# Ragged layer norm: per-batch tiles replaced by fixed tiles, gathered row pairs and scattered zeros

## Chip, cores, metric

One core of one Trainium2 chip. The metric is device time in microseconds (us), median over executions.

## The reference

```python
batch, max_seq, dim = (32, 512, 1024)
lengths = np.random.randint(64, max_seq, size=batch)
...
output = np.zeros_like(x)
for b in range(batch):
    seq_len = lengths[b]
    x_b = x[b, :seq_len].copy()
    mean = np.mean(x_b, axis=-1, keepdims=True)
    var = np.var(x_b, axis=-1, keepdims=True)
    output[b, :seq_len] = (x_b - mean) / np.sqrt(var + eps) * gamma + beta
```

Inputs and output are 32-bit floats; a row of 1024 is 4 KB. The draw is fixed: the lengths sum to 9,274 of 16,384 rows. The rest of the output must be zero.

## The kernel before

It works batch by batch: 512 rows as four groups of 128 partitions. Two groups are always loaded, the third and fourth only where the length asks for them. All four are computed; rows past the length get a scale of zero, and all 512 rows are stored.

```python
def st_load(b):
    ...
    nc.sync.dma_start(out=xs[:, 0 : G - 2, :], in_=xr[:, 0 : G - 2])
    nc.sync.dma_start(out=xs[:, G - 2, :], in_=xr[:, G - 2], cond=rv > (G - 2) * P)
    nc.sync.dma_start(out=xs[:, G - 1, :], in_=xr[:, G - 1], cond=rv > (G - 1) * P)
# per batch: bn_stats/bn_aggr on VectorE, sqrt on ScalarE, 1/std * mask and -mean/std on VectorE,
# h = x*rstd + nmr on ScalarE (16 bit), h *= gamma on VectorE,
# identity matmul of h plus (mask x beta) matmul into PSUM, one 128x2048 copy out on ScalarE
def st_store(b):
    ...
    for hf in range(NH):
        pool.dma_start(
            out=out[b].rearrange("(g p) d -> p g d", p=P)[:, hf * H : hf * H + H],
            in_=osb_q[b][hf][:, :, :],
        )
# the last three batches take a path without TensorE (NTAIL = 3)
```

## Time and profile before

| | before |
|---|---|
| median of the first 5 runs | 314.99 us (314.52 to 316.15) |
| span of the profiled run | 313.4 us |
| moved by DMA | 117.14 MB in 30,703 packets |
| ScalarE / VectorE busy | 86% / 83% |
| GB/s, 80 to 150 us | 420 |

The span runs from the first to the last instruction of the profiled execution; "DMA share" is the mean busy share of the core's 16 DMA engines and can exceed 1 where packets overlap. The lines of the page are in the prediction below, with how to read them.

### The profile page before, as it was taken

How to read it: one execution, taken by the hardware profiler on the slowest of the kernel's cores; microseconds unless marked ns; L12 is line 12 of the kernel's file. 1: busy time of each engine (PE TensorE's matmuls, PEld its weight loads, DVE VectorE, ACT ScalarE, POOL GpSimd, SP SyncE). 2: the span in 40 equal slices, each digit the busy share in tenths (PEclk: the TensorE clock that was granted, in tenths of full speed). 3: DMA queues.
4: the chain of work that ended last, by engine and by line, in shares of the span. 5: the costliest groups of instructions: out<-in, count | busy, mean ns of one | idle time of the engine just before them, and what ended most of it. 6: DMA issues, size and time to landing. Idle time of an engine off the chain costs nothing.

```text
span 313.4 us, 2482 instructions
## 1 busy us (share of the span) xinstructions
PE 212.5 (68%) x465; PEld 51.7 (16%) x465; DVE 260.1 (83%) x630; ACT 268.6 (86%) x231; POOL 52.6 (17%) x74
## 2 busy tenths in 40 slices
PE   0001433888888899888867888898688769845800
PEld 0000100222222222222211222122122212111200
DVE  4399999999999999999889987989797699716410
ACT  1007669999999999999889999998999899999990
POOL 8000001111111111111111111011111011131230
DMA  6999955999999999999999999999999997678987
GB/s 209 418 362 331 357 208 197 356 367 367 419 419 421 419 422 419 418 423 419 418 422 421 420 419 421 420 420 421 419 419 421 420 385 279 268 280 321 387 319 298
DMA packets 30703, 117.14 MB, mean 374 GB/s; under 512 B 2128, under 2 KB 2128, under 8 KB 30688
## 3 DMA queue, kind: packets, MB, share of 16 engines
q0 software_dynamic: 17440, 67.15, 53.3%
q1 hardware_dynamic: 13248, 49.84, 40.6%
q14 instruction: 12, 0.10, 0.1%
q8 instruction: 3, 0.05, 0.1%
HBM read 68.19 MB, written 67.11 MB: 432 GB/s over the span
## 4 chain that ended last, share of the span: by engine, by line
issue 56%; DVE 18%; POOL 12%; DMA 9%; ACT 2%; PE 1%; POOLq 1%; SPq 0%; ACTq 0%
POOL out_dram L275 12%; DVE stats L147 6%; DVE stats L148 6%; DMA out_dram<-o_sb 5%; DVE h_sb L203 4%; DMA x_all<-in_x_dram 3%; ACT h_sb L190 1%; DVE mv L149 1%; PE ps L219 1%; ACT o_sb L263 1%; POOLq L275 0%; POOLq L344 0%; DVE rstd L170 0%; DVE nmr L174 0%; SPq L59 0%
## 5 line engine op out<-in xcount | busy, mean ns | idle before, releaser
L219 PE MATMUL ps<-h_sb,idn_h 128*128 128x512 f16 x232 | 108.8, 624 | 70.5 <-ACT o_sb L263 46.9
L190 ACT ACTIVATE h_sb<-x_all,nmr,rstd 128x1024 f16<-128x1024 f32 x128 | 148.5, 1244 | 6.1 <-DVE nmr L174 6.1
L263 ACT ACTIVATE o_sb<-ps 128x2048 f32<-128x2048 f32 x58 | 106.5, 1878 | 6.8 <-DMA out_dram<-o_sb 6.7
L229 PE MATMUL ps<-beta_h,maskr 1*128 1x512 f16 x232 | 109.0, 622 | 0.0
L147 DVE BATCH_NORM_STATS2 stats<-x_all 128x6 f32<-128x512 f32 x128 | 86.3, 674 | 16.4 <-DMA x_all<-in_x_dram 16.4
L203 DVE TENSOR_TENSOR h_sb<-h_sb,gamma_h 128x1024 f16<-128x1024 f16 x128 | 82.5, 675 | 14.4 <-ACT h_sb L190 14.4
L275 POOL DMA_DIRECT2D out_dram<-o_sb x64 | 45.3, 708 | 243.0 <-ACT o_sb L263 185.1
L148 DVE BATCH_NORM_STATS2 stats<-x_all 128x6 f32<-128x512 f32 x128 | 84.0, 656 | 0.0
L219 PEld LDWEIGHTS <-idn_h 128*128 128x128 f16 x232 | 27.1, 128 | 149.6 <-issue 91.9
L229 PEld LDWEIGHTS <-maskr 1*128 1x128 f16 x232 | 24.4, 125 | 80.8 <-issue 80.8
L156 ACT ACTIVATE sq<-mv,eps_sb 128x4 f32<-128x4 f32 x32 | 9.5, 303 | 22.6 <-DVE mv L149 17.2
L149 DVE BATCH_NORM_AGGREGATE mv<-stats 128x2 f32<-128x12 f32 x128 | 25.3, 197 | 0.2
L251 ACT ACTIVATE o_sb<-h_sb,maskt 128x1024 f32<-128x1024 f16 x12 | 12.8, 1143 | 0.0
L109 PE MATMUL mtp<-idn_f,maskt 128*128 128x128 f32 x1 | 0.4, 444 | 15.3 <-DVE maskt L98 15.3
L207 DVE TENSOR_TENSOR h_sb<-h_sb,beta_h 128x1024 f16<-128x1024 f16 x12 | 8.3, 692 | 0.4
L170 DVE RECIPROCAL rstd<-sq 128x4 f32<-128x4 f32 x32 | 5.4, 168 | 3.5 <-ACT sq L156 3.5
L61 POOL MEMSET x_all<- 128x6144 f32 x1 | 5.2, 5218 | 0.3 <-POOLq L330 0.3
L174 DVE SCALAR_TENSOR_TENSOR nmr<-mv,rstd 128x4 f32<-128x4 f32 x32 | 4.7, 148 | 0.0
L79 DVE CAST lenf<-len 128x32 f32<-128x32 int32 x1 | 2.3, 2298 | 2.8 <-DMA len<-in_lengths_dram 2.8
L171 DVE TENSOR_TENSOR rstd<-rstd,maskt 128x4 f32<-128x4 f32 x32 | 4.6, 144 | 0.0
L109 PEld LDWEIGHTS mtp<-idn_f,maskt 128*128 128x128 f32 x1 | 0.2, 183 | 15.3 <-issue 15.3
L117 POOL DMA_DIRECT2D maskr<-masktr x1 | 0.7, 692 | 9.7 <-DVE masktr L113 9.7
(18 smaller groups left out, 6.3 us busy)
## 6 DMA issues: line engine op xcount, KB each, us to landing
out_dram<-o_sb POOLq DMA_DIRECT2D x64, 1024.0 KB, 12.4
x_all<-in_x_dram SPq DMA_DIRECT2D x30, 1024.0 KB
x_all<-in_x_dram SPq DMA_DIRECT2D x60, 512.0 KB
x_all<-in_x_dram SPq DMA_DIRECT2D x2, 2048.0 KB
gamma_f<-in_gamma_dram SPq DMA_DIRECT2D x1, 512.0 KB
beta_f<-in_beta_dram SPq DMA_DIRECT2D x1, 512.0 KB
len<-in_lengths_dram SPq DMA_DIRECT2D x1, 32.0 KB
maskr<-masktr POOLq DMA_DIRECT2D x1, 32.0 KB, 6.2
```

Of the source, the lines that this page charges most:

```text
L147: dve.bn_stats(out=stats[:, g, 0, :], in_=xg[:, 0 : D // 2])
L148: dve.bn_stats(out=stats[:, g, 1, :], in_=xg[:, D // 2 : D])
L149: dve.bn_aggr(out=mv[:, g, :], in_=stats[:, g].rearrange("p a b -> p (a b)"))
L156: act.activation(out=sq[:, :], in_=mv[:, :, 1], func=AF.Sqrt, bias=eps_sb[:, 0:1], scale=1.0,)
L190: act.activation(out=h_sb[b][:, g, :], in_=x_all[:, b % NBX, g, :], func=AF.Identity, bias=nmr[:, g : g + 1], scale=rstd[:, g : g + 1],)
L203: dve.tensor_tensor(out=hg, in0=hg, in1=gamma_h[:, :], op=OP.mult)
L207: dve.tensor_tensor(out=hg, in0=hg, in1=beta_h[:, :], op=OP.add)
L219: pe.matmul(ps[:, i, c * CH : (c + 1) * CH], idn_h[:, :], h_sb[b][:, g, c * CH : (c + 1) * CH], start=True, stop=False,)
L229: pe.matmul(ps[:, i, c * CH : (c + 1) * CH], maskr[0:1, b * G + g, :], beta_h[0:1, c * CH : (c + 1) * CH], start=False, stop=True,)
L251: act.activation(out=o_sb[:, i, :], in_=h_sb[b][:, g, :], func=AF.Copy, bias=0.0, scale=maskt[:, b, g : g + 1],)
L263: act.activation(out=o_sb[:, :, :].rearrange("p a b -> p (a b)"), in_=pst[hf][:, :, :].rearrange("p a b -> p (a b)"), func=AF.Copy, bias=0 ...
L275: pool.dma_start(out=out[b].rearrange("(g p) d -> p g d", p=P)[:, hf * H : hf * H + H], in_=osb_q[b][hf][:, :, :],)
```

## The change

The intent: touch only rows that count. The first 64 rows of every batch exist whatever the lengths, so they are loaded as eight fixed tiles of 256 rows (two adjacent rows per partition). All further valid rows are numbered as row pairs over all batches; VectorE computes from the running sum of the lengths which pair lies in which partition, and GpSimd gathers and scatters 128 pairs (1 MB) at a time. Padding is written by scattering one tile of zeros. Engines branch on the number of tiles. Instead of a tile framework's dependencies the kernel keeps its own semaphores. The diff replaces nearly the whole file; this is its core, with cuts marked by dots and remarks after # added here:

```diff
-        nc.sync.dma_start(out=xs[:, 0 : G - 2, :], in_=xr[:, 0 : G - 2])
-        nc.sync.dma_start(out=xs[:, G - 2, :], in_=xr[:, G - 2], cond=rv > (G - 2) * P)
-        nc.sync.dma_start(out=xs[:, G - 1, :], in_=xr[:, G - 1], cond=rv > (G - 1) * P)
...
+                    for t in range(NST):                      # 8 fixed tiles, SyncE
+                        e.dma_start(out=xt[t][:, :], in_=st_view(x, t)).then_inc(s_xs[t], 16)
...
+                    def load(t):                              # GpSimd
+                        d = t - NST
+                        e.indirect_dma_start(
+                            out=xt[t % RX][:, :], out_offset=None, in_=xu,
+                            in_offset=bass.IndirectOffsetOnAxis(ap=idx_i[:, d : d + 1], axis=0), ...
+                    def store(t):
+                        wait(tok["evac", t])
...
+                    KJ = [2, 3, 4, 5, 6, 10, 14, 18, 22]      # zero scatter j goes out in step KJ[j]
+                    while len(KJ) < NZ:
+                        KJ.append(27 + (len(KJ) - 9) // 2)
...
+        for k in range(NSTEP):
+            if k >= 2:
+                dve_mul(k - 2)
+            if k >= 1:
+                dve_smalls(k - 1)
+            dve_stats(k)
...                                                            # index, mask and zero arithmetic
+            if k >= 1:
+                act_xn(k - 1)
+            if k >= 2:
+                pe_mm(k - 2)
+                act_evac(k - 2)                                # two 128x1024 copies, scale = mask
+            act_sqrt(k)
...
+                    e.reg_mul(rz, rz, 16)
+                    e.wait_ge(s_zero, rz)                      # all zero scatters landed
+                    e.drain()
```

In step k VectorE takes the statistics of tile k, ScalarE normalises tile k-1, and tile k-2 goes through the product with gamma, the matmuls and the eviction (ScalarE's copy out of PSUM); GpSimd then stores it.

Ring sizes: eight load buffers (RX), six store buffers (RO), three 16-bit buffers (RH), two halves of PSUM.

## The prediction

> **What bounds the kernel now.** I read the page's busy shares first, then the row of forty slices, then the windows by stage, then the queue totals, then the groups and the timeline for durations.
>
> ```profile
> span 313.4 us, 2482 instructions
> PE 212.5 (68%) x465; PEld 51.7 (16%) x465; DVE 260.1 (83%) x630; ACT 268.6 (86%) x231; POOL 52.6 (17%) x74
> ...
> DMA  6999955999999999999999999999999997678987
> GB/s 209 418 362 331 357 208 197 356 367 367 419 419 421 419 422 419 418 423 419 418 422 421 420 419 421 420 420 421 419 419 421 420 385 279 268 280 321 387 319 298
> ```
>
> Three things are near their limit: VectorE, ScalarE and the transfers. A share of the span cannot tell which; the windows (columns: the stretch, busy time of each engine, clock, DMA share, GB/s) can.
>
> ```profile
> 7.80:80.00 72.20, 32.81 (x73) 8.40 (x73) 67.39 (x174) 49.54 (x47) 6.35 (x9) 1.00 0.90 331
> 80.00:150.00 70.00, 62.61 (x138) 15.01 (x137) 70.00 (x175) 70.00 (x60) 11.32 (x16) 1.00 1.02 420
> 150.00:265.00 115.00, 95.12 (x209) 23.06 (x209) 101.12 (x246) 108.19 (x91) 18.39 (x26) 1.00 1.01 413
> 265.00:313.40 48.40, 21.94 (x48) 5.20 (x47) 18.02 (x36) 39.63 (x35) 9.91 (x14) 1.00 0.77 304
> ```
>
> In the middle (80 to 265 us) the sixteen DMA engines are full at 413 to 420 GB/s. From 80 to 150 ScalarE has no gap either (70.00 of 70.00): a batch costs it 4.63 us of normalising plus 3.62 us of eviction in the timeline, 8.25 us, the period at which the chain shows the stores. After 150 both compute engines get gaps, so there the transfers alone set the pace. At both ends the transfers are underfed. The page's DMA total turns this into a sum: 117.14 MB at 420 GB/s is 278.9 us; the other 34.5 us of the span is lost at the ends: about 4 in the first 7.8 us, 15 up to 80 us (72.2 x (1 - 331/420)), 13 after 265 us (48.4 x (1 - 304/420)). So the kernel is bound by **bytes in the middle and by a bad start and end**.
>
> **What the Trainium skill says.** "DMA: Bandwidth & Descriptors", section "Issuing engines are not separate DMA queues": transfers started by any engine share the same 16 DMA engines. The trace agrees: loads (SyncE) and stores (GpSimd) together reach 420, while loads alone between 8 and 14 us reach 414 to 424. So moving loads to another issuer should neither win nor lose rate. "HBM Reference", section "Specifications (TRN2)": a core alone streams at about 425 GB/s; the trace's 420 is that ceiling, so only fewer bytes or a fuller queue can help. "Perfetto Trace Analysis", section "DMA Instruction — SWDGE (GPSIMD)": the profiled window of a GpSimd DMA is its descriptor generation, not the movement. The trace agrees: a store's window is 708 ns, its landing 12.4 us after issue. "SBUF — State Buffer", section "Who interferes with whom": a VectorE instruction in a two-port mode blocks GpSimd's descriptor writing. No view of the kernel before isolates this; I carry it as a risk.
>
> **The change, part by part.** *Bytes.* The draw is fixed; its lengths sum to 9,274 of 16,384 rows. The old kernel loads two whole batches, then 256, 384 or 512 rows of each by length: 11,904 rows, 48.8 MB, and stores all 67.1 MB. The new one loads 64 rows of every batch (8 fixed tiles of 256 rows) and gathers the rest as pairs of rows: 3,619 pairs in 29 tiles. Loads: 2,048 + 7,238 = 9,286 rows, 38.0 MB; stores of those 38.0 MB; 3,549 zero pairs scattered from one zero tile, 29.1 MB in 28 transfers; gamma's broadcast 0.5 MB. Sum 105.7 MB, **11.4 MB less**, which at 420 GB/s is 27 us.
>
> *Compute.* 37 tiles of 256 rows instead of 64, at these durations (groups; count, busy us and mean ns, idle):
>
> ```profile
> L190 ACT ACTIVATE h_sb<-x_all,nmr,rstd 128x1024 f16<-128x1024 f32 x128 | 148.5, 1244 | 6.1 <-DVE nmr L174 6.1
> L263 ACT ACTIVATE o_sb<-ps 128x2048 f32<-128x2048 f32 x58 | 106.5, 1878 | 6.8 <-DMA out_dram<-o_sb 6.7
> L203 DVE TENSOR_TENSOR h_sb<-h_sb,gamma_h 128x1024 f16<-128x1024 f16 x128 | 82.5, 675 | 14.4 <-ACT h_sb L190 14.4
> L275 POOL DMA_DIRECT2D out_dram<-o_sb x64 | 45.3, 708 | 243.0 <-ACT o_sb L263 185.1
> L251 ACT ACTIVATE o_sb<-h_sb,maskt 128x1024 f32<-128x1024 f16 x12 | 12.8, 1143 | 0.0
> ```
>
> Records overlap a little, so I use spacings from the timeline: normalising 1.16 us (4.63 for four), an eviction of 1024 with a mask scale 1.06 (4.25 for four of L251, its nearest relative), square root 0.2. ScalarE per step: 2 x 1.16 + 2 x 1.06 + 0.2 = **4.65 us**. The split eviction costs it 0.3 us a step against the old 1.81. VectorE: statistics with aggregation 1.26 us per 128 rows, twice, the gamma product 1.24 for 2048 (two old ones took that), small ones 0.3: **4.1 us**. TensorE: 8 matmuls spaced 0.43 to 0.46 us: 3.6. Over 39 steps (37 plus 2 to drain) ScalarE needs 181 us, VectorE 160 plus some 25 of new index and mask arithmetic. Both lie **beside** the transfers' 252 us, no longer level with them; this is what lets the queue stay full.
>
> *Steady steps.* A step moves one load and one store, 2.1 MB, plus a zero tile in one step of four: 5.0 to 5.6 us at 420 GB/s against 4.65 of ScalarE. Transfers bind, narrowly. From step 27 on, two zero tiles a step (19 in all) give 7.5 us of transfers per 4.65 us of compute, so the queue holds work after compute has ended: the old hollow end goes.
>
> *Start.* Eight fixed loads are issued at once: 9 MB, covering until about 24 us. VectorE first waits for the lengths (3.7 us) and the cast (2.3 us), then runs some 25 small instructions at 0.15 us and the first index chunk: step 0's statistics begin near 12 us, against 12.57 now. First normalising ends near 19 us, the first gather follows, in time. In steps 1 to 8 about 13 us of index, zero and mask arithmetic stretch VectorE's steps to 6 or 7 us; five early zero tiles fill in, 3 MB a step. I allow 5 us of underfed queue there.
>
> *Sum.* For the rate I take 410 GB/s: loads alone run at 420, but stores alone at the old end (304 to 310 us) at 385 to 410. 105.7 MB / 410 = 257.8 us; first transfer 2.5; underfed start 5; last landing and exit 3.5; timed run above span 1.6 (314.99 against 313.4). Total **270 us**.
>
> **The rivals.** *First, GpSimd's issuing becomes the bound.* It now issues 29 real gathers, 2 empty ones, 37 stores and 28 zero scatters, 96 in all, with branches and waits in program order. At the direct store's 0.71 us that is 68 us, no matter. At 2.8 us each it would equal 270 us; at 3.3, about 320. Against: the 708 ns for 256 row pieces; a gather has 128 pieces of 8 KB. For: an index read per piece, unmeasured here, and VectorE's port. *Second, scattered transfers on one queue run slower.* All but the first loads share GpSimd's queue. At 380 GB/s the sum is 291, at 350 it is 315: no change at all. Against: pieces double from 4 KB to 8 KB, neighbours are mostly adjacent in memory, and stores on that queue alone reach 410. *Third, the loads starve the pipeline.* A gather waits until its buffer was normalised and stands behind stores that wait for evictions; eight buffers give seven steps, 33 us or more, against a queue of up to 16 MB, 39 us. That loop fills the queue rather than emptying it, so I expect a few us: 275. *Fourth, the start is clean and the rate 420:* 252 + 8 = 260 us.
>
> **Range and chances.** Centre 270. Low end 258: rate 420 and only 6 us lost besides. High end 288: rate 385, or a start that loses 15 us more. Within 2% of 315 needs a rate near 355 or GpSimd at 3.2 us an issue: 0.03. Slower, GpSimd at 3.5 us or more: 0.04. Faster by over 2%: 0.93.
>
> **What would show each step right or wrong.** Queue totals: about 105.7 MB, nearly all on the software queue. Slices: 400 GB/s or more from the second to the second last, with a dip at most from 24 to 60 us. ScalarE near 181 us busy (65 to 70%), VectorE near 190, ScalarE's gaps ended by loads or store buffers. Matmul and statistics counts at 39/64 of two halves each. GpSimd's indirect windows at 1 to 1.5 us. After the last eviction, 15 to 30 us of zero stores alone. I am wrong if indirect windows exceed 2.7 us, if full slices show less than 390 GB/s, if the empty slices lie in the middle and end on waits for gathers, or if transfers stop well before the end.

## The result

| | before | after |
|---|---|---|
| median | 314.99 us (15 runs) | **268.27 us** (9 runs, 267.60 to 271.47) |
| ratio | | 0.8523 (0.8499 to 0.8546) |
| span profiled | 313.4 us | 267.1 us |
| DMA | 117.14 MB, 30,703 packets | 105.92 MB, 15,287 packets |
| ScalarE / VectorE / GpSimd busy | 86% / 83% / 17% | 66% / 68% / 43% |

A ratio is the mean time of one kernel's runs over that of the other's of the same rounds, so not quite the ratio of the medians. Executions over 1.5% slower than the fastest of the same kernel are left out of the means. 15% faster, and 1.7 us below the forecast. The forecast's range held; its terms did not all hold, as is shown below.

From the page of the kernel after, the lines that answer to those of before:

```profile
span 267.1 us, 1867 instructions
PE 137.0 (51%) x296; PEld 31.4 (12%) x296; DVE 181.8 (68%) x447; ACT 175.6 (66%) x191; POOL 113.6 (43%) x106
...
DMA  6999999999999999999999999999999999999930
GB/s 165 428 427 420 353 331 421 432 424 424 426 427 428 423 426 424 432 426 426 426 428 427 427 424 427 429 428 426 421 426 427 418 424 416 410 417 426 427 144 0
DMA packets 15287, 105.92 MB, mean 396 GB/s; under 512 B 2302, under 2 KB 2302, under 8 KB 2431
## 3 DMA queue, kind: packets, MB, share of 16 engines
q0 software_dynamic: 13824, 96.76, 87.1%
```

The hollow stretches of before (slices 3 to 10 and the last eight) are gone: from the second slice to the 38th the DMA engines are busy, and all but two of those slices are at 410 GB/s or more. The first slice, two dips (353 and 331) and the last two remain. The windows (columns as before: stretch, busy time by engine, clock, DMA share, GB/s) split it:

```profile
0.00:7.80 7.80, 0.00 (x0) 0.00 (x0) 3.67 (x28) 1.58 (x2) 2.67 (x10) 1.00 0.68 204
7.80:80.00 72.20, 37.04 (x80) 8.51 (x80) 61.32 (x153) 46.95 (x52) 27.06 (x25) 1.00 1.00 410
80.00:150.00 70.00, 48.01 (x104) 11.02 (x104) 56.06 (x129) 59.88 (x66) 34.08 (x30) 1.00 1.01 427
150.00:228.00 78.00, 51.94 (x113) 11.88 (x112) 60.76 (x140) 67.20 (x74) 48.85 (x41) 1.00 1.01 424
228.00:254.00 26.00, 0.00 (x0) 0.00 (x0) 0.00 (x0) 0.00 (x0) 0.97 (x1) 1.00 1.01 419
254.00:267.10 13.10, 0.00 (x0) 0.00 (x0) 0.00 (x0) 0.00 (x0) 0.00 (x0) 1.00 0.17 68
```

Four facts matter. Between 7.8 and 80 us the rate is 410 where it was 331. In the middle it is 427 where it was 420. From 228 us on no compute engine works, and zero scatters and late stores fill the queue for 26 us. And the last 13 us move almost nothing.

The groups, for the durations that the forecast had to guess (count, busy us and mean ns, idle before):

```profile
L336 ACT ACTIVATE h<-x,nmr,rstd 128x1024 f16<-128x1024 f32 x76 | 90.1, 1233 | 28.5 <-DVE nmr L316 28.1
L325 DVE BATCH_NORM_STATS2 stats<-x 128x6 f32<-128x512 f32 x156 | 96.1, 678 | 0.0
L344 ACT ACTIVATE o<-ps,mask 128x1024 f32<-128x1024 f32 x74 | 78.0, 1104 | 11.7 <-PE ps L366 6.8
L513 POOL DMA_INDIRECT x<-in_x_dram,idx_i x31 | 43.4, 1401 | 73.1 <-ACT h L336 55.0
L506 POOL DMA_INDIRECT out_dram<-o,idx_i x29 | 28.8, 993 | 28.6 <-ACT sq L351 26.9
L536 POOL DMA_INDIRECT out_dram<-zt,zidx_i x28 | 34.0, 1213 | 8.6 <-issue 7.7
```

The statistics (L325), first to touch a loaded tile, never waited for a load: idle 0.0. So loads do not pace the steps. What does is in the timeline (start, length, engine, line, what; idle before and its releaser in brackets), here ScalarE, then VectorE:

```profile
134.92 2.12 ACT L344 ACTIVATE o<-ps,mask 128x1024 f32<-128x1024 f32 x2 [0.15 <-PE ps L366]
136.93 0.29 ACT L351 ACTIVATE sq<-mv,eps_sb 128x2 f32<-128x2 f32 x1
137.65 2.37 ACT L336 ACTIVATE h<-x,nmr,rstd 128x1024 f16<-128x1024 f32 x2 [0.43 <-DVE nmr L316]
...
145.16 2.12 ACT L344 ACTIVATE o<-ps,mask 128x1024 f32<-128x1024 f32 x2 [0.15 <-PE ps L366]
```

```profile
137.26 0.17 DVE L315 RECIPROCAL rstd<-sq 128x2 f32<-128x2 f32 x1 [1.15 <-ACT sq L351]
137.46 0.16 DVE L316 SCALAR_TENSOR_TENSOR nmr<-mv,rstd 128x2 f32<-128x2 f32 x1
137.54 2.46 DVE L325 BATCH_NORM_STATS2 stats<-x 128x6 f32<-128x512 f32 x4
139.92 0.32 DVE L330 BATCH_NORM_AGGREGATE mv<-stats 128x2 f32<-128x12 f32 x2
140.16 1.20 DVE L309 TENSOR_TENSOR h<-h,gamma_h 128x2048 f16<-128x2048 f16 x1
```

and TensorE, up to the eviction at 145.16:

```profile
141.42 1.89 PE L360 MATMUL ps<-h,idn_h 128*128 128x512 f16 x4 [1.55 <-DVE h L309]
143.24 1.88 PE L366 MATMUL ps<-beta_h,ones_h 1*128 1x512 f16 x4
```

This is a loop through the engines: eviction, square root (in order behind it), reciprocal, statistics, gamma product, matmuls, next eviction. Two turns of ScalarE's row, 134.92 to 145.16, are two steps: **5.12 us a step**, though ScalarE, the busiest engine in such a step, works only some 4.8 of it (2.12 + 0.29 + 2.37). Steps with index, mask or zero arithmetic take 7 to 10 us; over the 36 steps from the first eviction (25.84 us) to the last (225.58) the mean is 5.55 us.

### The profile page after: what moved, and what is told of

It is laid out like the page before. It is cut to its first block, busy times and chain, and to the rows that moved or that the text cites.

```text
span 267.1 us, 1867 instructions
## 1 busy us (share of the span) xinstructions
PE 137.0 (51%) x296; PEld 31.4 (12%) x296; DVE 181.8 (68%) x447; ACT 175.6 (66%) x191; POOL 113.6 (43%) x106
## 2 busy tenths in 40 slices
DMA packets 15287, 105.92 MB, mean 396 GB/s; under 512 B 2302, under 2 KB 2302, under 8 KB 2431
## 3 DMA queue, kind: packets, MB, share of 16 engines
q0 software_dynamic: 13824, 96.76, 87.1%
## 4 chain that ended last, share of the span: by engine, by line
DVE 37%; PE 21%; ACT 16%; issue 9%; DMA 2%; POOL 0%; DVEq 0%; POOLq 0%; ACTq 0%; SPq 0%
DVE stats L325 17%; ACT o L344 12%; PE ps L360 11%; PE ps L366 10%; DVE h L309 7%; ACT h L336 3%; DMA len<-in_lengths_dram 2%; ACT sq L351 2%; DVE rstd L315 1%; DVE nmr L316 1%; DVE mv L330 1%; DVE prd L244 1%; DVE zcmp L286 1%; DVE zsum L288 1%; DVE idx_s L246 1%
## 5 line engine op out<-in xcount | busy, mean ns | idle before, releaser
L360 PE MATMUL ps<-h,idn_h 128*128 128x512 f16 x148 | 69.8, 627 | 88.5 <-DVE h L309 88.2
L336 ACT ACTIVATE h<-x,nmr,rstd 128x1024 f16<-128x1024 f32 x76 | 90.1, 1233 | 28.5 <-DVE nmr L316 28.1
L325 DVE BATCH_NORM_STATS2 stats<-x 128x6 f32<-128x512 f32 x156 | 96.1, 678 | 0.0
L344 ACT ACTIVATE o<-ps,mask 128x1024 f32<-128x1024 f32 x74 | 78.0, 1104 | 11.7 <-PE ps L366 6.8
L513 POOL DMA_INDIRECT x<-in_x_dram,idx_i x31 | 43.4, 1401 | 73.1 <-ACT h L336 55.0
L366 PE MATMUL ps<-beta_h,ones_h 1*128 1x512 f16 x148 | 69.7, 622 | 0.0
L309 DVE TENSOR_TENSOR h<-h,gamma_h 128x2048 f16<-128x2048 f16 x37 | 44.5, 1204 | 0.7 <-DVE zidx_i L291 0.7
L506 POOL DMA_INDIRECT out_dram<-o,idx_i x29 | 28.8, 993 | 28.6 <-ACT sq L351 26.9
L536 POOL DMA_INDIRECT out_dram<-zt,zidx_i x28 | 34.0, 1213 | 8.6 <-issue 7.7
L360 PEld LDWEIGHTS ps<-h,idn_h 128*128 128x128 f16 x148 | 16.0, 130 | 141.5 <-DVE h L309 119.8
```

The costliest lines, as they stand in the source:

```text
L309: tok["mul", t] = add("DVE", lambda: dve.tensor_tensor(out=h[:, :, :], in0=h[:, :, :], in1=gamma_h[:, None, :].broadcast_to([P, 2, D]), op ...
L325: tk = add("DVE", lambda j=j, c=c: dve.bn_stats(out=s[:, j, c, :], in_=xx[:, j * D + c * CH : j * D + c * CH + CH]), [load_dep(t)])
L336: tok["xn", t] = add("ACT", lambda j=j: act.activation(out=h[:, j, :], in_=xx[:, j * D : j * D + D], func=AF.Identity, bias=nmr[r][:, j : ...
L344: tok["evac", t] = add("ACT", lambda j=j: act.activation(out=o[:, j, :], in_=p_[:, j, :], func=AF.Copy, bias=0.0, scale=mask[:, t, j : j + ...
L360: add("PE", lambda j=j, c=c: pe.matmul(p_[:, j, c * CH : c * CH + CH], idn_h[:, :], h[:, j, c * CH : c * CH + CH], start=True, stop=False) ...
L366: tok["pe", t] = add("PE", lambda j=j, c=c: pe.matmul(p_[:, j, c * CH : c * CH + CH], ones_h[:, :], beta_h[:, c * CH : c * CH + CH], start ...
```

## The experiments

The changed kernel's final wait, against a register's value, could not be run again here, so the experiments wait against the constant 448 instead (28 zero scatters times 16) or, where said, on something else; const_wait is the control for that. Kernels were run in three groups, each on one chip with its own runs of the kernel before. "Against the control" is the difference of medians; for the second and third group the ratios carry the comparison. The diffs leave out allocations of extra tiles and semaphores, and mostly the change of the final wait.

| run | median us | ratio to before | against control | last eviction ends |
|---|---|---|---|---|
| const_wait | 269.34 | 0.8522 (0.8504 to 0.8539) | | 228.9 |
| no_drain | 272.89 | 0.8640 (0.8616 to 0.8664) | +3.6 | 228.9 |
| sqrt_first | 268.32 | 0.8498 (0.8469 to 0.8527) | -1.0 | 227.2 |
| zeros_late | 289.69 | 0.9166 (0.9143 to 0.9188) | +20.4 | 236.9 |
| bytes_11 | 295.20 | 0.9346 (0.9330 to 0.9361) | +25.9 | 252.6 |
| no_zeros (wrong) | 253.87 | 0.8044 (0.8031 to 0.8058) | -15.5 | 229.7 |
| act_more | 273.18 | 0.8657 (0.8642 to 0.8671) | +3.8 | 237.0 |
| pool_more | 270.65 | 0.8592 (0.8558 to 0.8626) | +1.3 | 233.2 |
| drain_early | 269.50 | 0.8535 (0.8522 to 0.8549) | +0.2 | 229.0 |
| drain_mid | 274.94 | 0.8706 (0.8692 to 0.8720) | +5.6 | 236.6 |
| early_and_sqrt | 268.65 | 0.8498 (0.8481 to 0.8515) | -0.7 | 227.2 |

**Control.**

```diff
-                    e.reg_mul(rz, rz, 16)
-                    e.wait_ge(s_zero, rz)
+                    e.wait_ge(s_zero, 28 * 16)
                     e.drain()
```

> Control: the changed kernel with its final wait on the zero scatters against a constant (448) in place of a register of the same value, since a register wait can't be rerun. Every theory: 268.3 us within 1 us, profile as before, with the long GpSimd drain after the last packet still there (span ends about 6.5 us after the last packet).

269.34 us, ratio 0.8522 against 0.8523: the same kernel. The difference of medians is the chip's (its runs of before read 315.9).

**Are bytes the price?** Eleven megabyte loads more, on SyncE's queue, one after the other, into a tile that nobody reads:

```diff
+                    e.wait_ge(s_xs[NST - 1], 16)
+                    for n in range(11):
+                        e.dma_start(out=spare[:, :], in_=st_view(x, n % NST)).then_inc(s_sp, 16)
+                        e.wait_ge(s_sp, 16 * (n + 1))
```

> Eleven more loads of 1 MB each into a spare tile, so that the bytes are those of the kernel before (117.4 MB). Theory A, bytes at 427 GB/s set the time: plus 27 us, 295 us; what is then left of the gain (315 to 295) is the fuller start and end. Theory B, compute or GpSimd's order sets it: plus 0 to 10 us.

295.20 us, 25.9 more than the control, for 11.5 MB: 445 GB/s for the added bytes, close to the queue's own 427. At equal bytes (117.45 against 117.14 MB) the new kernel is still 20 us faster than the old one. So of the gain, **some 26 us are fewer bytes and some 20 us a fuller queue**. The 20 us include the step from 420 to 427 GB/s, some 5 us at these bytes, whose reason no run isolates. The forecast had 27 us for bytes.

```profile
GB/s 165 429 425 369 321 414 426 425 428 429 428 423 425 426 423 425 426 425 425 428 425 426 428 425 428 428 428 425 426 424 425 421 424 425 420 420 425 425 266 2
```

From the sixth slice on the queue stayed full, and it now held compute up: evictions waited 26.3 us for store buffers (none in the kernel after), and the last one ended at 252.6 us.

**Do the early zero tiles carry weight?** The same 28 scatters, none before step 27:

```diff
-                    KJ = [2, 3, 4, 5, 6, 10, 14, 18, 22]
+                    KJ = []
                     while len(KJ) < NZ:
-                        KJ.append(27 + (len(KJ) - 9) // 2)
+                        KJ.append(27 + len(KJ) // 3)
```

> No zero scatter before step 27, three a step from there on. Theory A, the nine early zero tiles fill a queue that loads and stores alone don't fill (2.1 MB per 5.12 us is 410 GB/s, less during the first steps): 280 to 288 us, with slices under 410 GB/s between 24 and 170 us. Theory B, zero scatters hide wherever they stand: 268 within 2 us.

289.69 us, just above the range that I gave and 20.4 above the control. The slices (GB/s in fortieths of 287.7 us) show where:

```profile
GB/s 160 428 420 383 319 311 336 422 326 207 268 417 411 383 411 392 335 379 368 369 355 423 418 418 417 420 408 424 424 422 419 415 411 414 422 423 420 423 209 0
```

Slices 4 to 21 average about 355 although the evictions kept the control's pace through them. Nine megabytes of zeros without any dependency cost almost nothing while the queue has room, and 20 us when they come after it. This rejects the idea that scatters hide wherever they stand.

**What is left when the zeros go?** All scatters skipped:

```diff
                             e.reg_alu(rz, rz, 7, OP.arith_shift_right)
+                            e.reg_mul(rz, rz, 0)
...
-                    e.wait_ge(s_zero, rz)
-                    e.drain()
+                    for t in range(31, 37):
+                        e.wait_ge(s_o[t % RO], 16 * (t // RO + 1))
```

> All zero scatters skipped (the padding is then whatever the buffer held: wrong on purpose), no drain. Bytes fall to 76.8 MB, which alone would take 180 us. Theory A, compute's own loop (5.12 us a step, last eviction at 228 us) is the next bound, 28 us behind the transfers: 234 to 242 us. Theory B, transfers pace the steps too, so compute speeds up when they go: under 225 us.

The result is wrong (padding unwritten). The time, 253.87 us, missed my range of 234 to 242. The windows of this run, and below them two of the control's:

```profile
60.00:170.00 110.00, 75.10 (x163) 17.41 (x164) 86.03 (x193) 92.50 (x100) 46.53 (x39) 1.00 0.96 366
170.00:228.00 58.00, 39.67 (x86) 8.90 (x84) 46.96 (x109) 48.94 (x53) 16.21 (x15) 1.00 0.62 255
228.00:240.00 12.00, 0.00 (x0) 0.00 (x0) 0.00 (x0) 1.93 (x3) 0.97 (x1) 1.00 0.23 85
240.00:251.40 11.40, 0.00 (x0) 0.00 (x0) 0.00 (x0) 0.00 (x0) 0.00 (x0) 1.00 0.00 0
```

```profile
60.00:170.00 110.00, 75.95 (x165) 17.50 (x166) 86.80 (x196) 92.83 (x101) 50.08 (x44) 1.00 1.01 426
170.00:228.00 58.00, 38.84 (x84) 8.84 (x84) 46.18 (x107) 49.34 (x54) 39.99 (x34) 1.00 1.01 423
```

Theory A's core held: with 29 MB gone, loads and stores alone move only 366 GB/s, and the last eviction ends at 229.7, where it did before (228.9). Taking load off the queue made compute no faster, so the transfers do not pace the steps. A DMA share of 0.96 at 366 GB/s is also a warning: a share near 1 does not prove a full queue, for here the packets themselves lasted longer (8 KB ones 339 ns on average between 80 and 150 us, 310 in the control). What I had left out is the way out: after its last store (issued at 230.5) GpSimd walks the skipped zero blocks by compare-and-branch until 243.8, and then spends 5.63 us in a drain. In the full kernel the branches end at 246.3, beside the transfers; here they stick out.

**Does the steps' own loop matter?** The square root moved ahead of the evictions:

```diff
             if k >= 1:
                 act_xn(k - 1)
+            act_sqrt(k)
             if k >= 2:
                 pe_mm(k - 2)
                 act_evac(k - 2)
-            act_sqrt(k)
```

> ScalarE's square root of step k moved ahead of the evictions of tile k-2, which breaks the loop product, matmul, eviction, square root, statistics that paces a step at 5.12 us. Theory A, bytes set the time: compute ends about 10 to 16 us earlier (last eviction near 215 to 220 instead of 228 us), the time stays 268 within 2 us. Theory B, the step pace sets the time: 255 to 260 us.

268.32 us; the ratio's interval overlaps the control's. Where the loop alone had paced them, plain steps now took 4.7 us instead of 5.12, and the evictions of the 32nd tile began at 186.1 us, 15 us ahead of the control. The last one ended only 1.7 us earlier, not 10 to 16, because the last five tiles met a new wait:

```profile
ACT o L344 <- DMA out_dram<-o,idx_i: 16.2, 5, 3.7
```

(us in total, times, longest.) Evictions now wait for store buffers behind the zero backlog: what compute gained, the queue took back. The time did not follow the step pace, as theory A says; my number for compute's end was wrong.

**And in the other direction.** One more 128x1024 copy on ScalarE in each step:

```diff
             act_sqrt(k)
+            tok["junk", k] = add("ACT", lambda k=k: act.activation(out=junk[k % 2][:, :], in_=ones_w[:, :],
+                func=AF.Copy, bias=0.0, scale=1.0), [d_ow, tok.get(("junk", k - 2))])
```

> One idle 1024-wide copy more on ScalarE in each step (about 1.05 us, some 0.4 of it in the gap before the normalising, so a step of about 5.8 us; compute ends near 252 us). Theory A, the queue holds some 14 us of work in the middle (a load lands 14 us after issue) and absorbs it: 268 to 273 us. Theory B, the middle is paced by compute and the queue only just full: 280 to 293 us.

273.18 us, 3.8 above the control, just above theory A's range and below B's. The copies took 41.5 us in all, but much of that fell into the loop's gaps: a plain step grew from 5.12 to 5.39 us, not to 5.8, and the last eviction came 8 us later (237.0 us), not 24. So this run tests theory B less hard than planned. Of the 8 us the queue absorbed about half: it has a reserve, but not a deep one.

**GpSimd's room.**

```diff
+                        if k >= 3:
+                            e.wait_ge(s_pj, k - 2)
+                        e.memset(pjunk[k % 2][:, :], 0.0).then_inc(s_pj, 1)
                         if k >= 2:
                             store(k - 2)
```

> One memset of 128x1024 (about 0.9 us) more on GpSimd in each step. Theory A, GpSimd has slack (114 of 267 us busy): 268 within 1.5 us. Theory B, issuing is on the path: plus 15 to 33 us.

270.65 us with GpSimd busy for 147.6 instead of 113.6 us: 34 us more work, 1.3 us more time (2 by the ratio), slightly over what I allowed. Issuing is not on the path.

**The end.** After the last packet (260.6 us in the kernel after) the span runs on for 6.5 us. The records of the packed trace (the views of `prof` leave drains out) name one long instruction in that time, GpSimd's drain (the kernel's `e.drain()`): 7.92 us from 257.6 on. First trial, waits on the last six stores in its place, behind the wait on the zero scatters:

```diff
-                    e.drain()
+                    for t in range(31, 37):
+                        e.wait_ge(s_o[t % RO], 16 * (t // RO + 1))
```

> Final GpSimd drain replaced by constant waits on the last six stores' own semaphores and on the zero scatters. Theory A, the drain itself costs (trace: last packet at 260.6 us, drain ends 265.5, span 267.1): 263 to 265 us. Theory B, the drain only stands for write receipts that any wait must see: 268 within 1 us.

272.89 us, slower by 3.6: both my numbers missed. The records show why. The block's end drains GpSimd anyway; that drain now began at 261.1, after everything had landed, and again lasted 7.92 us. In the control it had begun at 258.4, beside the last three us of transfers. So the drain itself takes the time, and this edit only started it later. Second trial, the drain first and those waits behind it:

```diff
+                    e.drain()
+                    e.wait_ge(s_zero, 28 * 16)
+                    for t in range(31, 37):
+                        e.wait_ge(s_o[t % RO], 16 * (t // RO + 1))
-                    e.wait_ge(s_zero, 28 * 16)
-                    e.drain()
```

> The GpSimd drain moved ahead of the final waits (which are then on the zero scatters and the last six stores, as constants), so that it runs while the zero backlog still moves. Theory A, the drain is work of GpSimd's own, as long as the count of GpSimd transfers issued since the last drain (7.92 us for 96, 5.63 us for 68): the drain record still lasts 7.9 us but starts near 247 us and ends before the last packet; span ends about 2 us after the last packet, 264 to 266 us against 269.3 of the control. Theory B, the drain waits for the transfers: it lasts until the last packet and what follows is unchanged, 268 to 273 us.

269.50 us: no gain. The drain began at 248.2, lasted 17.4 us and ended at 265.5, 4.3 us after the last packet (261.2). So it does wait for transfers in flight, and outlasts them all the same. Third, an additional drain at step 20:

```diff
+                        if k == 20:
+                            e.drain()
                         if k >= 2:
                             store(k - 2)
```

> The control with one more drain at step 20 (some 44 transfers issued by then). Theory A, 82 ns for each transfer since the last drain: the middle drain lasts about 3.6 us, the last one about 4.3 us instead of 7.92; the time falls by 3 to 4 us against 269.3, if the middle stop of GpSimd is absorbed. Theory B, a fixed cost of the last drain: it stays at 7.92 us.

274.94 us, 5.6 worse. The middle drain held GpSimd for 14.5 us (131.9 to 146.4), no transfer was issued behind it meanwhile, and the queue ran dry:

```profile
132.00:142.00 10.00, 7.40 (x16) 1.70 (x16) 7.91 (x19) 9.00 (x11) 1.39 (x1) 1.00 1.01 424
142.00:148.00 6.00, 3.87 (x9) 0.98 (x10) 4.86 (x10) 5.43 (x7) 0.76 (x1) 1.00 0.09 40
```

The last drain fell to 5.15 us. Neither theory as I wrote it holds: the drain is not fixed, but 82 ns for each transfer, which fits 7.92 us after 96 transfers and 5.63 after 68 (no_zeros), would give 4.1 us for the 50 issued behind the middle drain. What part of it could be avoided stays open. Of the placements tried, the kernel's own is as good as any.

**Best version.** The edits of drain_early and of sqrt_first together:

> Early drain and square root ahead of the evictions together. Bytes theory: the second adds at most 1 us, 263 to 265 us, the best version of this study.

268.65 us, above my 263 to 265, since the early drain brings nothing; ratio 0.8498, the same as sqrt_first alone. Neither is clearly better than the changed kernel.

## Why the prediction was right

By its own steps:

- **Bytes.** 105.7 MB forecast, 105.92 measured, 96.76 of them on the software queue. That they are the price is shown by bytes_11.
- **The rate.** The forecast took 410 GB/s; the queue ran at 427. At that rate the bytes take 248.1 us, not 257.8: this term was 9.7 us too long, and the old kernel's 420 was not the ceiling that the prediction took it for. Stores alone at the old kernel's end were a poor guide; 228 to 254 us in the new one shows mainly stores at 419. Median packets last 309 ns for 8 KB and 159 ns for 4 KB, so two small ones cost 9 ns more; that the larger pieces made 427 out of 420 fits this, but no run isolates it.
- **First transfer.** 2.5 us allowed; the first slice, at 165 GB/s, falls short of 427 by 4.1 us.
- **The start.** 5 us allowed for a queue underfed by VectorE's arithmetic; the two dips cost 2.7 us, and only the first of them has the forecast reason. The second gather, behind VectorE's arithmetic of 17.4 to 20.9 us, was issued at 25.55 us, not in time: counting what was issued against what the packets had moved, 0.4 MB was left at 26.9 us, before its window ended (0.1 MB at 28.0 us in the control). In the second dip, 36 to 40 us, at least 2.7 MB were issued and not yet moved, yet packets took up to 1.8 us; that one stays open. Once the early zeros flow, from 29 us on, they cover the later arithmetic, as zeros_late shows by taking them away (207 and 268 GB/s in its slices 10 and 11, 424 and 426 in the kernel after).
- **The end.** 3.5 us allowed for last landing and exit; the last two slices fall short by 11.1 us: 4.4 in which the rate runs down (the DMA share falls from 0.96 at 253 us to 0.02 at 260), and 6.7 of exit, most of it under the drain. This was the largest term left out, 7.6 us, and the kernel before could have warned: its records hold a GpSimd drain too, 7.47 us up to 312.6, but beside the last stores, only 0.9 us beyond the last packet.
- **The sum.** 9.7 and 2.3 too much, 1.6 and 7.6 too little, some 1.2 us of other small dips: the near hit is partly luck. The mechanism, bytes over a full queue, is shown; the sizes of start, rate and end offset each other.
- **Compute beside the transfers.** Right in its consequence: ScalarE 175.6 us busy (181 forecast), VectorE 181.8, and after the last eviction 26 us of transfers at full rate (15 to 30 forecast), 33 us to the last packet. Wrong in the step "Transfers bind, narrowly", with ScalarE at 4.65 us and its gaps ended by loads or store buffers. The steps pace themselves at 5.12 us by the loop through the engines, ScalarE's gaps end on VectorE's small instruction (28.1 of them), and loads and stores alone leave the queue at 366 GB/s (no_zeros). **It is the zero scatters, put where there is room, that keep it full**, not a balance of load, store and compute. sqrt_first shows that a faster step gains nothing here, act_more that about half of a slower one is paid for (3.8 of 8 us), zeros_late that the time hangs on the fillers.
- **The rivals.** GpSimd's issue: 1.40 us for a gather, 0.99 and 1.21 for scatters, about the 1 to 1.5 forecast (the longest 2.0, under the 2.7 named as a sign of being wrong); pool_more leaves it off the path. Whether VectorE's port, carried as a risk, lengthened single windows, no run isolates. Slower scattered transfers: refuted by 427 GB/s. Starving loads: refuted by L325's 0.0.

## What to carry to other kernels

When transfers set the time, count bytes first, then ask what the queue has to do in every stretch; work that depends on nothing, such as writing zeros, is best spent where dependent transfers leave the queue short and at the end behind the last computation. A faster step is worth nothing while a backlog stands behind it. And look at what the program does after its last packet: here 6.5 us lay there that no busy row shows.

## What the Trainium skill lacked or had wrong

- "VectorE: DVE Perf Modes", section "The DRAIN you can't avoid", knows VectorE's own flushes and the runtime's boilerplate drains on all five engines, at about 12 ns, constant. The drains seen here are the program's, a third kind: GpSimd's lasted 34 to 188 ns where no transfer had been issued since the last one, 7.92 us after 96 GpSimd transfers (the same in the eight runs where it began after the zero scatters had landed) and 5.63 us after 68. Begun at 248.2 us with transfers in flight, it ended 4.3 us after the last packet. No page that I read tells of this cost.
- "DMA: Bandwidth & Descriptors", section "Anatomy of one DMA — SWDGE (gpsimd) path", calls descriptor generation small and gives no figure for indirect transfers. For 128 pieces of 8 KB GpSimd was held 1.40 us by a gather and 0.99 us by a scatter, against 0.59 us by a direct store of the same size.
- No page explains it: at 28 to 40 us packets of 8 KB took up to 1.8 us against a median of 0.31. Without the fillers such packets come later too: 112 of over 0.9 us in no_zeros, up to 173 us, against 21 in the control. Why is open.
